# The MLP's output product in a two-layer encoder kernel: seven half-size products by Strassen's scheme in place of eight

## The chip, the cores and the metric

The kernel runs on one NeuronCore of a Trainium2 chip. The metric is device time in microseconds (us) of one execution; a run is one execution, and the median of three runs is shown. A profile is one further execution taken by the hardware profiler. Engines: PE is TensorE (matmuls), DVE is VectorE, ACT is ScalarE, POOL is GpSimd, SP is SyncE, which here only issues DMAs.

## The reference

Two post-norm layers over x (1024 tokens by 1024 features, float32). Each layer is a mixer (gated linear plus differential attention, or windowed attention), a cross-attention into a memory, and a gated MLP with a causal convolution of width 3 on its gate. The change is in the MLP, whose second matmul is the output product:

```python
def conv_ffn(x, w_in, conv_w, conv_b, w_out):
    g, u = jnp.split(x @ w_in, 2, axis=-1)
    g = causal_depthwise_conv(g, conv_w, conv_b)
    h = jax.nn.gelu(g.astype(f32)) * u.astype(f32)
    return h.astype(x.dtype) @ w_out
...
        h = conv_ffn(x, ffn_w_in[i], ffn_conv_w[i], ffn_conv_b[i], ffn_w_out[i])
        x = layer_norm(DEEPNORM_ALPHA * x + h, ln_g[i, 2], ln_b[i, 2])
```

Here h is 1024 x 2816 and w_out is 2816 x 1024, for each of two layers.

## The kernel before, in words

**Precision by splitting.** Every matmul operand is split into a high and a low part (`split`, lines 113 to 115: ACT casts the source to the high part at line 114, DVE subtracts it from the source at line 115), and each product of two tiles is three matmuls: high by high, high by low, low by high.

**The MLP's first half: the gate and up product.** The hidden width is 22 chunks of 128, numbered j (`FF = 22`). `ffn_gen` (from line 354) makes for each j the gate and the up rows by a Strassen scheme already: seven products named P1 to P7, each of 12 matmuls of 512 columns, so 84 matmuls for one j. `seq` fixes the order of the products; `prep` (operand sums on DVE at line 385, then a split) runs up to six products ahead of `prod` (matmuls, lines 419 to 421), held by eight operand tiles rb. `post` empties PSUM, applies the convolution (`tap`, line 431) and the gelu, and multiplies (line 466) into a hidden tile h of 128 x 1024. Two h buffers take turns; they, and other scratch, are parts ("slots") of `acc`, the tile that otherwise holds x. Line 468 stores each h to DRAM (`hid`). `load` (line 377) fetches two raw weight tiles for each j, two j ahead, into four tiles, as soon as the last split that reads the old ones is done.

**The second half: the output product.** `ffn` walks two groups g of 512 tokens. For each g it walks the 22 j: `out_prep` loads a row of w_out (512 KB) and half of hid[j] (256 KB), and splits both; then, for each of four token tiles, `mm` (lines 553 to 555) runs three matmuls for each of two halves of the columns: 24 matmuls of 512 columns for one (g, j). PSUM has eight banks; all eight hold sums through a group. `evac` adds the result to ALPHA * x, and a layer norm follows. The last `LAST = 5` j of the second group are taken tile by tile, so that the norms of the last four tiles lie beside matmuls.

**What sets the order.** The program is written in one sequence, but a scheduler places each engine's instructions by its own estimate of when they can run. So the order on an engine is not the order in the text: an instruction whose inputs are early stands early. Each engine, and SP's DMA queue, then works strictly in that order on the chip.

Of the kernel before, what the change touches and what calls it, by code (L numbers as in the profile page):

```python
# [8 lines left out]
F32 = mybir.dt.float32  # L9
F32R = mybir.dt.float32r  # L10
# [7 lines left out]
P = 128  # L18
# [47 lines left out]
class Net:  # L66
    def __init__(s, tc, ctx, I, wlist):
        s.tc, s.nc, s.I = tc, tc.nc, I
        nc = s.nc
        cp = ctx.enter_context(tc.tile_pool(name="const", bufs=1))  # L70
        s.ident = cp.tile([P, P], F32, name="ident")
        s.nhalf = cp.tile([P, 4], F32, name="nhalf")

        pad = cp.tile([P, 88], F32, name="pad")
        nc.gpsimd.memset(pad[:, 0:1], 0.0)
        s.xh = cp.tile([P, NK, T], F32R, name="xh")
        s.xl = cp.tile([P, NK, T], F32R, name="xl")
# [9 lines left out]
        nc.gpsimd.memset(s.tiny("pad2", 88, 1)[:, 0:1], 0.0)  # L87
# [268 lines left out]
    def ffn_gen(s, l):  # L356

        nc = s.nc
        FF = s.FF
        cw = s.sm.tile([P, FF, 4], F32, name="cw", tag="cw", bufs=1)  # L360
        nc.sync.dma_start(out=cw, in_=s.I["conv"][l])
        accf = s.acc.rearrange("p t d -> p (t d)")
# [74 lines left out]

        def post(j, b):
            x, q = X[j], j % 2
# [21 lines left out]
            else:  # L461
# [7 lines left out]
                del X[j], raw[j]  # L469

        load(0, 0)
        load(0, 1)
# [16 lines left out]
        for i, (j, b) in enumerate(seq):  # L489
# [2 lines left out]
                dd += [s.d2(), s.d2()]  # L492
            prod(j, b)
            post(j, b)
            ahead(min(i + 6, 8) if i < 4 else i + 6)
            if i in (1, 3):
                yield
            if j == FF - 1 and b == "P2":
                s.xs.close()
                s.open_x(s.GU)  # L500
                s.out_start(l)
            elif j == FF - 1 and b in ("P3", "P7", "P4"):
                s.out_prep(("P3", "P7", "P4").index(b))
        yield


    LAST = 5

    def out_start(s, l):
        s.bl, s.bn, s.bu = l, 0, {}  # L510
        s.bseq = [(g, j) for g in range(2) for j in range(s.FF)]

    def out_prep(s, upto):
        nc = s.nc
        while s.bn < len(s.bseq) and s.bn <= upto and s.R.n() >= 3:
            g, j = s.bseq[s.bn]
            s.bn += 1
            st = s.stg.tile([P, T], F32, name="st", tag="st")
            nc.sync.dma_start(out=st, in_=s.I["ffn_out%d" % s.bl][j * P:(j + 1) * P, :])
            c = s.fc()  # L520
            nc.sync.dma_start(out=c, in_=s.hid[j][:, 512 * g:512 * g + 512])
            w, lo, u = s.R.get(), s.R.get(), s.R.get()
            s.split(u[:, 0:512], u[:, 512:T], c)
            s.split(w, lo, st)
            s.bu[g, j] = (w, lo, u)

    def evac(s, t, ps, tot):

        if not isinstance(ps, list):
            return s.acc_add(t, ps, True, tot)  # L530
        tt = s.tiny("tt", 2)
        for hf in range(2):
            c = slice(hf * 512, hf * 512 + 512)
            s.nc.vector.scalar_tensor_tensor(out=s.acc[:, t, c], in0=s.acc[:, t, c], scalar=ALPHA, in1=ps[hf],
                                             op0=ALU.mult, op1=ALU.add, accum_out=tt[:, hf:hf + 1])
        s.nc.vector.tensor_tensor(out=tot, in0=tt[:, 0:1], in1=tt[:, 1:2], op=ALU.add)

    def ffn(s, l, out=None, keep=None):
        nc = s.nc
        FF, L = s.FF, s.LAST  # L540
        s.load_ln(l, 2)
        late = []

        def mm(t, ps, js):
            po = ps if isinstance(ps, list) else [ps[:, 0:512], ps[:, 512:1024]]
            sl = slice((t % 4) * P, (t % 4) * P + P)
            for hf, o in enumerate(po):
                c = slice(hf * 512, hf * 512 + 512)
                for j in js:
                    w, lo, u = s.bu[t // 4, j]  # L550
                    hh, hl = u[:, 0:512], u[:, 512:T]
                    z = dict(skip_group_check=True)
                    nc.tensor.matmul(o, hh[:, sl], w[:, c], start=j == 0, stop=False, **z)  # L553
                    nc.tensor.matmul(o, hh[:, sl], lo[:, c], start=False, stop=False, **z)  # L554
                    nc.tensor.matmul(o, hl[:, sl], w[:, c], start=False, stop=j == FF - 1, **z)  # L555
# [6 lines left out]
        for g in range(2):  # L562
            ps = [s.d2(), s.d2(), [s.s1(), s.s1()], [s.s1(), s.s1()]]
            for j in range(FF - (L if g else 0)):
                s.out_prep(g * FF + j)
                for i in range(4):
                    mm(4 * g + i, ps[i], [j])
                s.R.put(*s.bu.pop((g, j)))
                s.out_prep(g * FF + j + 4)
                if 2 <= g * FF + j < 10:  # L570
                    t = g * FF + j - 2
                    nc.sync.dma_start(out=s.acc[:, t, :], in_=s.xres[t * P:(t + 1) * P, :])
                if late and j >= 1:
                    t, tot = late.pop(0)
                    s.ln(t, tot)
                    done(t)
            if g == 0:
                for t in range(4):
                    tot = s.tot()
                    s.evac(t, ps[t], tot)  # L580
                    late.append((t, tot))
        s.out_prep(2 * FF)
        s.hold = False
        xq = list(range(6))
        for i in range(4):
            t = 4 + i
            mm(t, ps[i], range(FF - L, FF))
            if i == 3:
                for j in range(FF - L, FF):
                    s.R.put(*s.bu.pop((1, j)))  # L590
            s.w_emit()
            tot = s.tot()
            if out is not None:
                s.last_tile(t, ps[i], tot, out)
                continue
            s.evac(t, ps[i], tot)
            s.ln(t, tot)
            done(t)
            for _ in range(2 * i):
# [3 lines left out]
            s.xtq = xq + [6, 7]  # L603
        s.drop_ln()

    def last_tile(s, t, ps, tot, out):

        nc = s.nc
        s.evac(t, ps, tot)
        g = s.ln_gen(t, tot, 1 if t < NT - 1 else 2)  # L610
        mu = next(g)
        if s.lag:
# [1020 lines left out]
```

## Time and profile before

| | |
|---|---|
| median of three runs | 2806.81 us (2803.17 to 2809.97) |
| the profiled execution's own time | 2802.9 us |
| its span, first to last instruction | 2801.2 us |
| PE, DVE, ACT, POOL busy, share of the span | 98%, 65%, 43%, 4% |
| granted TensorE clock, mean | 0.993 |
| DMA, mean over the span | 100 GB/s |

A busy share is the share of the span in which the engine had an instruction running. Matmuls overlap one another (each is drawn as lasting 389 ns), so a busy PE says that PE never waited, and how fast it goes is read from the spacing of the matmuls. "Idle before, releaser" is the time an engine stood still before an instruction, and what let it go on.

### The profile page before, as it was taken

The page shows a single profiled execution, that of the slowest core. Times are in us where ns is not written, and L with a number is a line of the kernel's source. Part 1 is how long each engine was busy: PE and PEld are TensorE (multiplying, and loading weights), DVE is VectorE, ACT ScalarE, POOL GpSimd, SP SyncE. Part 2 cuts the span into 40 slices and gives each one's busy share as a digit, 9 for nine tenths or more (in the row PEclk, how much of TensorE's full clock was granted, in tenths as well). Part 3 has the DMA queues.
Part 4 walks back from the last instruction along what each step waited for, and adds up shares of the span by engine and source line. Part 5 has one row for each costly group of instructions (what it writes and reads, how often), then busy time and mean ns, then how long its engine had stood idle before and what let it go on. Part 6 is the DMA issues. An engine that isn't in the chain of part 4 may idle for free.

```text
span 2801.2 us, 38176 instructions
## 1 busy us (share of the span) xinstructions
PE 2740.6 (98%) x14616; PEld 2304.2 (82%) x14616; DVE 1819.5 (65%) x3359; ACT 1192.9 (43%) x2303; POOL 105.3 (4%) x115
## 2 busy tenths in 40 slices
PE   8999999999999999999999999999998999999998
PEld 7778887899987888888887777789996888888887
DVE  4547665755589777764446787575569777775354
ACT  4325554433245444433333566343336444443232
POOL 0000000100010000000000000000000000000010
PEclk9999999999999999999999999999999999999999
DMA  3113313422213222226453323332212222226452
GB/s 130 39 48 94 103 48 94 132 83 82 69 56 111 76 85 89 75 102 218 147 173 121 103 56 99 98 100 82 76 53 98 89 86 76 90 83 210 143 174 96
DMA packets 94473, 279.12 MB, mean 100 GB/s; under 512 B 15026, under 2 KB 15315, under 8 KB 94291
## 3 DMA queue, kind: packets, MB, share of 16 engines
q1 hardware_dynamic: 92928, 274.87, 30.6%
q8 instruction: 115, 1.88, 0.3%
q10 hardware_dynamic: 1362, 1.81, 0.2%
q14 instruction: 68, 0.55, 0.1%
HBM read 212.67 MB, written 40.89 MB: 91 GB/s over the span
## 4 chain that ended last, share of the span: by engine, by line
PE 74%; DVE 4%; ACT 1%; DMA 1%; issue 1%; POOL 0%; DVEq 0%; SPq 0%; ACTq 0%; POOLq 0%
PE d L419 6%; PE d L420 6%; PE d L421 6%; PE s L421 4%; PE s L420 4%; PE s L419 4%; PE s L553 3%; PE s L554 3%; PE s L555 3%; PE d L554 3%; PE d L553 3%; PE d L555 3%; PE s L261 2%; PE s L714 2%; PE s L716 2%; PE s L715 2%
## 5 line engine op out<-in xcount | busy, mean ns | idle before, releaser
L114 ACT CAST rb<-st 128x1024 fp32r<-128x1024 f32 (+2 forms) x179 | 159.2, 890 | 260.8 <-issue 84.4
L115 DVE TENSOR_TENSOR rb<-st,rb 128x1024 fp32r<-128x1024 f32 (+2 forms) x179 | 182.1, 1018 | 114.4 <-ACT rb L114 106.5
L419 PE MATMUL s<-xh,rb 128*128 128x512 f32 x528 | 205.7, 389 | 0.0
L421 PE MATMUL s<-xh,rb 128*128 128x512 f32 x528 | 205.4, 389 | 0.0
L420 PE MATMUL s<-xl,rb 128*128 128x512 f32 x528 | 205.4, 389 | 0.0
L148 PE MATMUL s<-xh,rb 128*128 128x512 f32 x416 | 166.1, 399 | 1.5 <-DVE xl L115 1.5
L149 PE MATMUL s<-xl,rb 128*128 128x512 f32 x416 | 162.9, 392 | 0.0
L150 PE MATMUL s<-xh,rb 128*128 128x512 f32 x416 | 162.8, 391 | 0.0
L164 POOL TENSOR_TENSOR lnrs<-lnrs,nhalf 128x1 f32<-128x1 f32 x48 | 70.9, 1482 | 2209.8 <-DVE lnrs L163 2209.8
L431 DVE SCALAR_TENSOR_TENSOR fc<-f,cw,fc 128x512 f32<-128x512 f32 x176 | 132.2, 751 | 31.4 <-ACT fc L429 28.7
L714 PE MATMUL s<-gu,xh 128*128 128x256 f32 x512 | 144.6, 282 | 0.0
L114 ACT CAST rb<-acc 128x512 fp32r<-128x512 f32 (+1 forms) x124 | 83.1, 671 | 144.2 <-PE d L420 128.0
L716 PE MATMUL s<-gu,xl 128*128 128x256 f32 x512 | 143.5, 280 | 0.0
L715 PE MATMUL s<-gu,xh 128*128 128x256 f32 x512 | 143.4, 280 | 0.0
L115 DVE TENSOR_TENSOR rb<-acc,rb 128x512 fp32r<-128x512 f32 (+1 forms) x124 | 92.4, 747 | 63.3 <-ACT rb L114 62.8
L261 PE MATMUL s<-xh,rb 128*128 128x512 f32 x448 | 128.7, 398 | 3.5 <-ACT xh L114 1.1
L419 PEld LDWEIGHTS s<-xh,rb 128*128 128x128 f32 x528 | 99.2, 188 | 20.6
L421 PEld LDWEIGHTS s<-xh,rb 128*128 128x128 f32 x528 | 99.1, 188 | 20.6
L420 PEld LDWEIGHTS s<-xl,rb 128*128 128x128 f32 x528 | 99.1, 188 | 20.6
L441 DVE TENSOR_TENSOR acc<-s,acc 128x512 f32<-128x512 f32 x120 | 82.3, 686 | 43.4 <-PE s L421 43.3
L114 ACT CAST rb<-tmp 128x512 fp32r<-128x512 f32 x88 | 54.7, 624 | 129.6 <-PE d L420 119.9
L115 DVE TENSOR_TENSOR rx<-st,rx 128x1024 fp32r<-128x1024 f32 x70 | 85.7, 1225 | 29.0 <-ACT rx L114 28.7
(406 smaller groups left out, 7837.7 us busy)
## 6 DMA issues: line engine op xcount, KB each, us to landing
st<-in_ffn_out_dram SPq DMA_DIRECT2D x88, 512.0 KB, 3.7
st<-in_ffn_in_dram SPq DMA_DIRECT2D x44, 512.0 KB, 3.5
hid<-acc SPq DMA_DIRECT2D x44, 512.0 KB, 2.6
fc<-hid SPq DMA_DIRECT2D x88, 256.0 KB, 2.7
st<-in_mem_kv_dram SPq DMA_DIRECT2D x32, 512.0 KB, 3.8
f<-in_ffn_in_dram SPq DMA_DIRECT2D x22, 512.0 KB, 3.5
acc<-in_ffn_in_dram SPq DMA_DIRECT2D x22, 512.0 KB, 3.5
st<-in_memT_dram SPq DMA_DIRECT2D x16, 512.0 KB, 3.6
```

The source lines that it names most:

```text
L114: s.nc.scalar.copy(out=hi, in_=src)
L115: s.nc.vector.tensor_tensor(out=lo, in0=src, in1=hi.bitcast(F32), op=ALU.subtract)
L261: nc.tensor.matmul(ps[hf], a[:, c], b[:, hf * 512:hf * 512 + 512], start=st, stop=sp)
L419: nc.tensor.matmul(o, h[:, k, :], bh[:, q, :], start=first and k == 0, stop=False, **z)
L420: nc.tensor.matmul(o, h[:, k, :], bl[:, q, :], start=False, stop=False, **z)
L421: nc.tensor.matmul(o, lo[:, k, :], bh[:, q, :], start=False, stop=k == 3, **z)
L553: nc.tensor.matmul(o, hh[:, sl], w[:, c], start=j == 0, stop=False, **z)
L554: nc.tensor.matmul(o, hh[:, sl], lo[:, c], start=False, stop=False, **z)
L555: nc.tensor.matmul(o, hl[:, sl], w[:, c], start=False, stop=j == FF - 1, **z)
L714: nc.tensor.matmul(o, s.xh[:, k, sl], gh, start=k == 0, stop=False)
L715: nc.tensor.matmul(o, s.xh[:, k, sl], gl, start=False, stop=False)
L716: nc.tensor.matmul(o, s.xl[:, k, sl], gh, start=False, stop=k == NK - 1)
```

## The change

The output product h @ w_out is cut in two in each of its three directions: tokens, hidden width (chunk m against chunk m + 11) and columns. Seven products of half-size blocks replace eight. With A for h and B for w_out, the products are P1 = A11 B11, P6 = S2 T2, P2 = A12 B21, P7 = S3 T3, P5 = S1 T1, P3 = S4 B22, P4 = A22 T4; the S are four sums of blocks of h, the T four sums of blocks of w_out.

Each product walks 11 chunks m, each chunk is 12 matmuls of 512 columns (four token tiles, three matmuls), and needs one block of A and one of B, loaded into one tile of 128 x 1024 and split once. The seven products use the eight PSUM banks in two sets of four (A and B in `ffn`), and `post` adds their parts into x.

The sums are made during the gate and up product, on GpSimd (`gsum`), eight for each m and so 88 for each layer, 128 x 512 each. Hidden chunks are now visited in pairs (m, m + 11), by the table `jo`. Four tiles `wr` receive blocks of w_out. Results go to DRAM (`sa`, `sb`) by SP, each store written two products behind its sum in the text.

```diff
-                nc.sync.dma_start(out=s.hid[j], in_=h)
...
+        wr = {(0, 0): slot(12), (0, 1): slot(13), (1, 0): s.p1x[0], (1, 1): s.p1x[1]}
+        WS = (3, 5, 7, 8, 9, 11, 13, 14, 15, 17, 19)
...
+        def gsum(dst, o, x, y, op=ALU.subtract):
+            nc.gpsimd.tensor_tensor(out=o, in0=x, in1=y, op=op)
+            stores.append((dst, o))
...
+        def side(j, b):
+            m = j // 2
+            if b == "P5":
+                if j:
+                    raw_store(j - 1)
+                if j and j % 2 == 0:
+                    h_sums(m - 1)
+                if j in WS:
+                    w_load(WS.index(j))
+            if b == "P4" and j in WS or b == "P1" and j - 1 in WS or b in ("P2", "P7") and j and j % 2 == 0:
+                s.sa_store(2)
+            if b == "P2" and j in WS:
+                w_sums(WS.index(j))
...
+        def h_sums(m):
+            d = s.sa[m]
+            a11, a21, a12, a22 = (x[:, c:c + 512] for x in hs for c in (0, 512))
+            s1 = s.fc()
+            gsum(d["S1"], s1, a21, a22, ALU.add)
+            gsum(d["S3"], a21, a11, a21)
+            gsum(d["S2"], a11, s1, a11)
+            gsum(d["S4"], a12, a12, a11)
...
+        def w_sums(m):
+            d = s.sb[m]
+            b11, b12, b21, b22 = wr.values()
+            gsum(d["T1"], b11, b12, b11)
+            gsum(d["T3"], b12, b22, b12)
+            gsum(d["T2"], b22, b22, b11)
+            gsum(d["T4"], b21, b21, b22)
...
-    LAST = 5
+    LAST = 7
+    OUTS = (("P1", "A11", (0, 0)), ("P6", "S2", "T2"), ("P2", "A12", (1, 0)), ("P7", "S3", "T3"), ("P5", "S1", "T1"),
+            ("P3", "S4", (1, 1)), ("P4", "A22", "T4"))
...
+            st = s.bst[s.bn % len(s.bst)]
+            nc.sync.dma_start(out=st[:, 0:512], in_=s.sa[m][a])
...
+            nc.sync.dma_start(out=st[:, 512:T], in_=w)
+            hi, lo = s.R.get(), s.R.get()
+            s.split(hi, lo, st)
...
+            for m in ms:
+                hi, lo = s.bu[p, m]
+                w, wl = hi[:, 512:T], lo[:, 512:T]
+                nc.tensor.matmul(ps[i], hi[:, c], w, start=first and m == 0, stop=False, **z)
+                nc.tensor.matmul(ps[i], hi[:, c], wl, start=False, stop=False, **z)
+                nc.tensor.matmul(ps[i], lo[:, c], w, start=False, stop=last and m == H - 1, **z)
...
+            if b == "P1":
+                for o in (right(i), left(t), right(t)):
+                    add(o, ps[i], ALPHA)
```

**SP's queue in the gate and up product.** This is SP's order in layer 0, early in the gate and up product, before and after; `in_ffn_in` loads are the raw weight tiles that PE's products need, `hid`, `saA`, `saS` and `sbT` are stores, `in_ffn_out` loads feed the T sums. Before:

```order
L468 DMA hid2_97<-acc_64 128x1024
L377 DMA st_7372<-in_ffn_in_dram 128x1024
L377 DMA st_7373<-in_ffn_in_dram 128x1024
L468 DMA hid3_98<-acc_64 128x1024
L377 DMA f0_4810<-in_ffn_in_dram 128x1024
```

After, one round of T sums (loads, then stores that wait for their sums), with the loads between:

```order
L520 DMA p1x1_7468<-in_ffn_out_dram 128x512
L385 DMA f0_4909<-in_ffn_in_dram 128x1024
L520 DMA p1x0_7467<-in_ffn_out_dram 128x512
L571 DMA sbT14_188<-acc_64 128x512
L571 DMA sbT34_190<-acc_64 128x512
L571 DMA sbT24_189<-p1x1_7468 128x512
L571 DMA sbT44_191<-p1x0_7467 128x512
L520 DMA acc_64<-in_ffn_out_dram 128x512 x2
L520 DMA p1x1_7468<-in_ffn_out_dram 128x512
L520 DMA p1x0_7467<-in_ffn_out_dram 128x512
L385 DMA acc_64<-in_ffn_in_dram 128x1024
```

The scheduler has moved the rounds of T sums far ahead of where the text has them: the stores of S4 for the first, second, third and fourth pair of chunks have 1, 15, 30 and 44 stores of T sums before them, so all of them stand ahead of the fourth of eleven pairs, and the raw loads stand behind stores that wait for sums.

**GpSimd's queue in the gate and up product.** There was nothing here before but one memset; now, in layer 0 between the first and the second pair's sums (fc is S1 of a pair, the rows that write p1x are T2 and T4):

```order
L483 TENSOR_TENSOR acc_64<-acc_64 128x512
L483 TENSOR_TENSOR acc_64<-p1x1_7468,acc_64 128x512
L483 TENSOR_TENSOR p1x1_7468<-p1x1_7468,acc_64 128x512
L483 TENSOR_TENSOR p1x0_7467<-p1x0_7467,p1x1_7468 128x512
L483 TENSOR_TENSOR fc_8742<-acc_64 128x512
L483 TENSOR_TENSOR acc_64<-acc_64 128x512
L483 TENSOR_TENSOR acc_64<-fc_8742,acc_64 128x512
```

Rounds of four T sums follow each other, with the four S sums of a pair between.

**DVE's queue where the last product begins.** In layer 0 the norms of the first token tiles (L182, L185 before; L185, L188 now) stand beside the last splits (L115; L118). Before, the last splits and the first of the last four tiles:

```order
L115 TENSOR_TENSOR rx7_10813<-st_12216,rx6_10812 128x1024
L115 TENSOR_TENSOR rb0_70<-st_12224,rb7_77 128x1024
L115 TENSOR_TENSOR rb5_75<-st_12262,rb4_74 128x1024
L205 SCALAR_TENSOR_TENSOR acc_64,tot_12270<-acc_64,d2_11634 128x1024
L115 TENSOR_TENSOR rb1_71<-st_12266,rb6_76 128x1024
```

After, with the norms of the first three tiles between the splits (tt8 rows: P3's last parts added from PSUM):

```order
L613 SCALAR_TENSOR_TENSOR acc_64,tt8_11224<-acc_64,d2_11980 128x512
L166 TENSOR_SCALAR lnrs_12360<-lnrs_12360 128x1
L185 SCALAR_TENSOR_TENSOR acc_64<-acc_64,lnmu_12359,f1_4910 128x1024
L118 TENSOR_TENSOR rx1_11140<-st_11146,rx0_11139 128x1024
L188 SCALAR_TENSOR_TENSOR acc_64<-acc_64,lnrs_12360,f2_4911 128x1024
L118 TENSOR_TENSOR rx3_11142<-rp0_11137,rx2_11141 128x1024
L166 TENSOR_SCALAR lnrs_12388<-lnrs_12388 128x1
L185 SCALAR_TENSOR_TENSOR acc_64<-acc_64,lnmu_12387,f1_4910 128x1024
L118 TENSOR_TENSOR rx5_11144<-rp1_11138,rx4_11143 128x1024
```

Seven splits of the last product now share DVE with four norms, where the norms of the first four tiles had a whole group of 22 steps before.

## Rows read from the trace of the kernel before

**Rows 1.** The page, part 1 (busy time) and part 2 (PE over 40 slices).
```profile
span 2801.2 us, 38176 instructions
PE 2740.6 (98%) x14616; PEld 2304.2 (82%) x14616; DVE 1819.5 (65%) x3359; ACT 1192.9 (43%) x2303; POOL 105.3 (4%) x115
```
**Rows 2.** Windows: gate and up product, then three of layer 0's output product.
```profile
1000.00:1020.00 20.00, 20.00 (x90) 16.54 (x89) 15.20 (x24) 8.66 (x15) 0.00 (x0) 1.00 0.24 79
...
1270.00:1300.00 30.00, 30.00 (x134) 24.85 (x133) 14.07 (x16) 9.63 (x12) 0.00 (x0) 1.00 0.90 312
1300.00:1340.00 40.00, 40.00 (x178) 33.13 (x177) 14.34 (x16) 12.57 (x16) 0.00 (x0) 1.00 0.42 142
...
1480.00:1510.00 30.00, 29.61 (x147) 23.70 (x146) 22.00 (x35) 13.63 (x21) 4.34 (x3) 1.00 0.30 106
```
**Rows 3.** Whom PE waited for, 860 to 1267 us (the whole answer).
```profile
PE d L419 <- ACT acc L448: 0.2, 1, 0.2
```
**Rows 4.** DVE by line, gate and up product, 860 to 1250 us.
```profile
L441 DVE TENSOR_TENSOR acc<-s,acc 128x512 f32<-128x512 f32 x57 | 39.1, 686 | 15.4 <-PE s L421 15.4
L115 DVE TENSOR_TENSOR rb<-acc,rb 128x512 fp32r<-128x512 f32 x55 | 37.7, 686 | 24.4 <-ACT rb L114 24.4
L466 DVE TENSOR_TENSOR acc<-fc,acc 128x512 f32<-128x512 f32 x42 | 28.8, 689 | 1.8
```
**Rows 5.** GpSimd's line 164: duration min/median/max; then the timeline around 1404 us.
```profile
L164 POOL TENSOR_TENSOR dms<-dms,nhalf x32: 537/542/1384, 238.0 to 510.8; 128x1 f32<-128x1 f32 x32
...
1403.62 1.27 DVE L182 SCALAR_TENSOR_TENSOR acc<-acc,lnmu,f 128x1024 f32<-128x1024 f32 x1
1403.85 3.19 POOL L164 TENSOR_TENSOR lnrs<-lnrs,nhalf 128x1 f32<-128x1 f32 x1 [2.20 <-DVE lnrs L163]
1404.82 0.68 DVE L115 TENSOR_TENSOR rx<-fc,rx 128x512 fp32r<-128x512 f32 x1
1405.42 1.21 DVE L115 TENSOR_TENSOR rx<-st,rx 128x1024 fp32r<-128x1024 f32 x1
1407.07 1.28 DVE L185 SCALAR_TENSOR_TENSOR acc<-acc,lnrs,f 128x1024 f32<-128x1024 f32 x1 [0.44 <-POOL lnrs L164]
```
**Rows 6.** GpSimd by line and form: its only wide instructions, memsets.
```profile
L1143 POOL MEMSET gaT<- 32x1024 f32 x1 | 0.9, 942 | 0.1
L1148 POOL MEMSET fc<- 128x128 f32 x1 | 0.2, 213 | 0.0
```
**Rows 7.** The page, part 6: issues, KB each (all of a group), us to landing.
```profile
st<-in_ffn_in_dram SPq DMA_DIRECT2D x44, 512.0 KB, 3.5
hid<-acc SPq DMA_DIRECT2D x44, 512.0 KB, 2.6
fc<-hid SPq DMA_DIRECT2D x88, 256.0 KB, 2.7
```
**Rows 8.** SP's timeline, 934 to 964 us; then DVE's around 1004 us.
```profile
943.24 0.33 SPq L377 DMA_DIRECT2D acc<-in_ffn_in_dram  x1
...
953.49 9.11 SPq L377 DMA_DIRECT2D st<-in_ffn_in_dram  x2
...
1004.69 0.69 DVE L385 TENSOR_TENSOR tmp<-st 128x512 f32<-128x512 f32 x1 [1.18 <-DMA st<-in_ffn_in_dram]
```
**Rows 9.** DVE and ACT by line, layer 0's output product, 1267 to 1520 us.
```profile
L115 DVE TENSOR_TENSOR rx<-st,rx 128x1024 fp32r<-128x1024 f32 x32 | 39.2, 1225 | 9.9 <-ACT rx L114 9.8
L185 DVE SCALAR_TENSOR_TENSOR acc<-acc,lnrs,f 128x1024 f32<-128x1024 f32 x8 | 10.1, 1277 | 0.9 <-POOL lnrs L164 0.9
L534 DVE SCALAR_TENSOR_TENSOR acc<-acc,s 128x512 f32<-128x512 f32 x8 | 5.2, 681 | 0.1
...
L114 ACT CAST rx<-st 128x1024 fp32r<-128x1024 f32 x30 | 31.4, 1046 | 3.8 <-DMA st<-in_ffn_out_dram 2.4 <-DVE rx L115 1.4
```
**Rows 10.** The end of the span: PE's last matmul, DVE's last instructions.
```profile
2792.05 0.39 PE L555 MATMUL s<-rb,rb 128*128 128x512 f32 x1
...
2796.34 1.41 DVE L185 SCALAR_TENSOR_TENSOR acc<-acc,lnrs,f 128x512 f32<-128x512 f32 x2
```

More of the change, by code (lines that the diff above doesn't have):

```diff
@@ L359, in ffn_gen @@
         FF = s.FF
+        H = FF // 2
+        jo = [m + H * i for m in range(H) for i in range(2)]
         cw = s.sm.tile([P, FF, 4], F32, name="cw", tag="cw", bufs=1)
@@ L513, in out_prep @@
     def out_prep(s, upto):
         nc = s.nc
-        while s.bn < len(s.bseq) and s.bn <= upto and s.R.n() >= 3:
-            g, j = s.bseq[s.bn]
+        while s.bn < len(s.bseq) and s.bn <= upto and s.R.n() >= 2:
+            p, m = s.bseq[s.bn]
             s.bn += 1
[L518 to L536, printed above, removed]
+            _, a, b = s.OUTS[p]
@@ L539, in ffn @@
         nc = s.nc
-        FF, L = s.FF, s.LAST
+        H, L = s.FF // 2, s.LAST
         s.load_ln(l, 2)
         late = []
[L544 to L555, printed above, removed]
+        tt = [s.tiny("tt8", 2, 8) for _ in range(NT)]
@@ new lines, in ffn, with add, mm @@
+        left, right = (lambda t, c=c: s.acc[:, t, c:c + 512] for c in (0, 512))
+        stt = nc.vector.scalar_tensor_tensor
+        def add(o, x, al=1.0, tot=None):
+            stt(out=o, in0=o, scalar=al, in1=x, op0=ALU.mult, op1=ALU.add, accum_out=tot)
+        def mm(ps, i, p, ms):
+            first, last = s.OUTS[p][0] in ("P1", "P5", "P6"), s.OUTS[p][0] in ("P2", "P3", "P4")
+            c = slice(i * P, i * P + P)
+            z = dict(skip_group_check=True)
+            for m in ms:
[4 more added lines that the diff above has]
+                nc.tensor.matmul(ps[i], lo[:, c], w, start=False, stop=last and m == H - 1, **z)
@@ L559, in done @@
             nc.sync.dma_start(out=dst[t * P:(t + 1) * P, :], in_=s.acc[:, t, :])
-        s.lag = None
[L562 to L565, printed above, removed]
-                for i in range(4):
[L567 to L575, printed above, removed]
-                    done(t)
[L577 to L581, printed above, removed]
@@ L582, in ffn, with total, post @@
-        s.out_prep(2 * FF)
+        def total(t):
+            tot = s.tot()
+            nc.vector.tensor_tensor(out=tot, in0=tt[t][:, 0:1], in1=tt[t][:, 1:2], op=ALU.add)
+            return tot
+        def post(b, ps, i):
+            t = 4 + i
+            if b == "P1":
+                for o in (right(i), left(t), right(t)):
+                    add(o, ps[i], ALPHA)
+            elif b == "P6":
+                add(right(i), ps[i])
+            elif b == "P2":
+                add(left(i), ps[i], ALPHA, tt[i][:, 0:1])
+            elif b == "P7":
+                add(right(t), ps[i])
+            elif b == "P5":
+                add(right(t), ps[i], 1.0, tt[t][:, 1:2])
+            elif b == "P3":
+                add(right(i), ps[i], 1.0, tt[i][:, 1:2])
+                late.append(i)
+            else:
+                add(left(t), ps[i], 1.0, tt[t][:, 0:1])
@@ new lines, in ffn @@
+        s.lag = None
+        A = None
+        B = [s.s1() for _ in range(4)]
+        for p, (b, _, _) in enumerate(s.OUTS):
+            if b in ("P1", "P5"):
+                A = [x[:, c:c + 512] for x in (s.d2(), s.d2()) for c in (0, 512)]
+            ps = B if b in ("P6", "P7", "P4") else A
+            for m in range(H - (L if b == "P4" else 0)):
+                s.out_prep(p * H + m)
+                for i in range(4):
+                    mm(ps, i, p, [m])
+                    if m == H - 1:
+                        post(b, ps, i)
+                s.R.put(*s.bu.pop((p, m)))
+                s.out_prep(p * H + m + 4)
+                if p == 0 and m in (2, 5):
+                    s.sa_store(2)
+                if p == 0 and m >= 2:
+                    for t in ((0,), (1,), (2,), (3,), (6,), (7,), (4,), (5,), ())[m - 2]:
+                        nc.sync.dma_start(out=s.acc[:, t, :], in_=s.xres[t * P:(t + 1) * P, :])
+                if late and m < H - 1:
+                    t = late.pop(0)
+                    s.ln(t, total(t))
+                    done(t)
@@ L583, in ffn @@
+        assert not late and not s.stores
+        s.out_prep(7 * H)
         s.hold = False
```

63 lines of the change are left out of this document (45 added, 18 removed).

## The prediction, made before the changed kernel had run

> **What bounds the kernel now.** I read the busy times first: PE is busy for 2740.6 of 2801.2 us, the next engine, DVE, for 65%, and GpSimd for 4% [rows 1]. Then the waits of PE: over a whole gate and up product it waited 0.2 us [rows 3]. Then the windows, for the pace: 178 matmuls of 512 columns lie in 40 us at a granted clock of 1.00, and as each is drawn 0.39 us long, the pace is (40 + 0.39) / 178 = 0.2269 us for each [rows 2]. So both MLP stages are bound by the number of matmuls, and a matmul taken away is worth 0.227 us, as long as what feeds PE keeps up.
>
> **Matmuls removed.** Before: 22 chunks x 8 tiles x 2 halves x 3 = 1056 for each layer. After: 7 products x 11 x 4 x 3 = 924. Over two layers 264 fewer, of the same shape: 264 x 0.2269 = **59.9 us saved**. This is all there is to gain; the rest of the working is about what is given back.
>
> **The output stage's feeding.** One chunk is now 12 x 0.2269 = 2.72 us of PE. It needs one cast of 1.05 us on ACT and one subtraction of 1.23 us on DVE [rows 9], two DMA issues of 0.33 us on SP [rows 8], and 2 x 256 KB of DMA. DMA moved 312 GB/s at a busy share of 0.90 [rows 2], so 347 GB/s full: 524 KB take 1.5 us. Every feeder has over a microsecond to spare, and loads stand four chunks (11 us) ahead of a landing of 2.7 us [rows 7]. The densest stretch is P1, which also takes in x: about 16 tiles' worth of 524 KB and 1.6 MB of late stores in 30 us are 333 GB/s, just under 347, so I cost it at nothing; if it doesn't fit, the four chunks of lead cover a lag of a few us. At P1's end DVE adds 12 parts from PSUM, 12 x 0.68 = 8.2 us [rows 9], against two or three chunks already split (5.4 to 8.2 us): nothing, up to 3 us a layer.
>
> **The norms in the last product.** Seven splits at 1.23 and three norms at 2 x 1.28 [rows 9] take DVE 16.3 us after P3 ends, while PE has four chunks, 10.9 us, and then tiles whose later chunks need the last splits; PE's new order takes two tiles' early chunks first, another 5 us. About 0.5 us a layer is left. At layer 0's end each of the last four tiles now gives 21 x 0.227 = 4.8 us of matmuls for a norm instead of 6.8, and DVE was already busy for 22.0 of 30 us there [rows 2]: I put down 1 us. Behind the last matmul the same chain of one addition and one norm follows as before (9 us to the end of the span) [rows 10]. Together **2 us given back**, bounds 0 and 8.
>
> **The sums on GpSimd.** 88 a layer, and the scheduler puts 43 of the T sums and 12 S sums between the first and the fourth pair of chunks: 55 in six chunks, nine for each. A chunk is 84 x 0.2269 = 19.1 us. No row shows such a sum. From below it costs what DVE takes for the same size, 0.69 us [rows 4]. From above: GpSimd's memsets grow by (942 - 213) / 896 = 0.81 ns an element [rows 6]; three streams of 512 make 1.25 us, plus the 0.54 of its smallest two-input instruction [rows 5], 1.8 us. I take 1.25 us.
>
> By the Trainium skill (GPSIMD Engine Reference, § 3.1) a two-input element costs about 2.6 cycles at 1.2 GHz, an estimate of 1.1 us; the sum would be the same.
>
> Two things can come of it. First, **DVE's time**. It is busy 15.2 of 20 us [rows 2], so 4.6 us of a chunk are free. Rows 5 show that the two engines get in each other's way: an instruction of 0.54 us on GpSimd lasted 3.19 us while three DVE instructions with two inputs in SBUF ran back to back, and ended 0.4 us behind them. DVE lost nothing there (1.27, 0.68, 1.21 us are its usual times), but that GpSimd instruction had one element to read. A sum reads 512, and while it reads, DVE may stand. DVE's loss for each sum lies between 0 and 1.8 us; with DVE busy 76% of the time a sum of 1.25 us displaces 0.95. Over six chunks: 55 x 0.95 = 52 us against 6 x 4.6 = 28 free and six products of lead before PE feels it, 6 x 2.72 = 16: 8 us for each layer.
>
> Second, **SP's queue**. It is in order, and raw loads stand behind stores that wait for sums, which DVE meets soon after: one load landed 1.2 us later than DVE wanted it even before [rows 8]. A round is four sums, then a store issued, and a load that lands in 2.7 us [rows 7]: 4s + 3.8 us for a sum of s. Two chunks hold 3.6 rounds and four S sums, 18.4 s + 13.7 us, against 38.1: even at s = 1.33. Stretched by DVE to 1.7, three pairs lose 21 us, less 16 of lead: 4 us a layer.
>
> Both eat the same lead, and a DVE that waits for a load leaves GpSimd free, so I take **10 us a layer**, between 8 and the sum of both.
>
> **Sum.** 2802.9 (the profiled execution) - 59.9 + 2 + 2 x 10 = 2765 us. The median of the runs shown lies 3.9 us above the profiled time; I leave the forecast at **2765**. Two runs of this kernel differ by about 0.2%, so less than that (5.6 us) counts as the same.
>
> **Rivals.**
> *Everything is hidden* (the lead and DVE's free time hold): 2802.9 - 59.9 + 3 = 2746. For it: DVE lost nothing in rows 5. Against it: nine sums a chunk against 4.6 free microseconds.
> *SP's queue is the bound*: sums stretch as the 3.19 us row did, to 2.1 us; then two chunks take 52.3 us of the queue, 14.2 too many, 43 over three pairs, 27 after the lead, 54 for two layers, less what a waiting DVE gives back, say half: 2803 - 60 + 2 + 40 = 2785. It decides from s = 1.33 + 16 / 55 = 1.6 us.
> *DVE becomes the bound, and the change is slower*: each sum takes the reading path for its whole length and DVE stands for 1.6 us. Then 55 x 1.6 = 88, less 28 and 16, is 44 a layer: 2803 - 60 + 2 + 88 = 2833. It turns slower than before from a loss of 1.33 us a sum, (44 + 29) / 55. For it: all of DVE's instructions in this stage but the additions from PSUM (line 441, first of rows 4) have two inputs in SBUF, the kind that held GpSimd up in rows 5. Against it: 1.6 is more than a sum is likely to last.
> The Trainium skill has this as a rule (SBUF — State Buffer, § Who interferes with whom): a DVE instruction with two SBUF inputs and a GpSimd one that reads SBUF exclude each other, and the second to issue waits for the whole of the first. The trace agrees for GpSimd as the second (3.19 us for 0.54); no row shows DVE as the second.
> That the matmuls are not fewer is no rival: PE's order holds 1848 of them where it held 2112.
>
> **Numbers.** Forecast (2752 to 2774) 0.42; everything hidden 0.19; SP's queue (2774 to 2801) 0.20; DVE the bound (above 2801) 0.15; the other 0.04 is a stall of the output stage (2774 to 2790). The range 2742 to 2803 leaves out most of the slower case and little below. Within 0.2% of before lies the edge between SP's queue and DVE as the bound, 0.03 of each: the same 0.06. Faster: 0.42 + 0.19 + 0.17 + 0.04 = 0.82. Slower: 0.12.
>
> **What would show it.** In the profile after: PE's spacing still 0.227 us in the output product, and 1848 matmuls there; the window from the first S sum to the fourth pair with a PE below full and waits for the splits behind it, while later chunks show 0; GpSimd's sums near 1.25 us alone and 1.5 to 2 beside DVE; DVE's two-input instructions stretched beyond 0.69, its PSUM ones not; raw loads issued later than 9 us apart. I am wrong if PE waits for the last product's splits for more than 2 us a layer, if P1 waits for DMA, or if sums last over 2 us.

## The result, and the profile after

The changed kernel took 2821.25 us (median; 2818.80 to 2823.52), the kernel before beside it 2806.26: a ratio of **1.0052, 95% interval 1.0038 to 1.0067**. By the bound of 0.2% it is **slower**, by 15 us, where 2765 (2742 to 2803) had been forecast. The profiled execution took 2823.5 us, with a span of 2821.8 against 2801.2 [rows 1].

First the output product itself. These are the first and the last of its matmuls on its first line, in layer 0 and in layer 1, before and then after (durations min/median/max in ns, then the first and last start):

```profile
L553 PE MATMUL d<-rx,rx x88: 389/389/396, 1267.5 to 1491.5; 128*128 128x512 f32 x88
L553 PE MATMUL s<-rb,rb x4: 389/397/400, 1498.2 to 1511.9; 128*128 128x512 f32 x4
...
L553 PE MATMUL d<-rx,rx x88: 389/389/393, 2552.6 to 2776.6; 128*128 128x512 f32 x88
L553 PE MATMUL s<-rb,rb x4: 389/389/389, 2781.4 to 2791.6; 128*128 128x512 f32 x4
```
```profile
L622 PE MATMUL d<-rx x108: 388/389/504, 1303.3 to 1487.3; 128*128 128x512 f32 x108
L622 PE MATMUL s<-rb x8: 389/394/486, 1503.2 to 1518.7; 128*128 128x512 f32 x8
...
L622 PE MATMUL d<-rx x108: 388/389/504, 2599.7 to 2783.3; 128*128 128x512 f32 x108
L622 PE MATMUL s<-rb x8: 389/389/397, 2799.2 to 2812.0; 128*128 128x512 f32 x8
```

It went from 1511.9 - 1267.5 = 244.4 to 1518.7 - 1303.3 = 215.4 us in layer 0, and from 239.0 to 212.3 in layer 1: **55.7 of the 59.9 us are there.** But it starts 35.8 us later in layer 0. From its end there to its start in layer 1 another 40.3 us were added (1081.0 against 1040.7). With 0.2 us more behind the last matmul that is the whole difference: 35.8 - 29.0 + 40.3 - 26.7 + 0.2 = 20.6 us of span. So the time was lost ahead of the output product, where PE had waited for next to nothing before [rows 3].

The windows tell in which part of the gate and up product. The columns are busy time and instructions of PE, PEld, DVE, ACT and POOL, the granted clock, the DMA share and GB/s. First the changed kernel's layer 0, from the start of the product on, and layer 1's product; then the kernel before:

```profile
860.00:900.00 40.00, 39.55 (x175) 32.30 (x173) 39.61 (x55) 20.90 (x34) 9.25 (x7) 1.00 0.35 119
900.00:1060.00 160.00, 135.16 (x549) 109.12 (x548) 132.11 (x152) 55.43 (x92) 78.94 (x53) 0.91 0.64 220
1060.00:1140.00 80.00, 80.00 (x355) 66.26 (x354) 67.57 (x93) 35.60 (x58) 12.21 (x8) 1.00 0.29 100
1140.00:1270.00 130.00, 130.00 (x576) 107.66 (x575) 109.91 (x149) 59.26 (x96) 22.54 (x15) 1.00 0.30 104
2140.00:2560.00 420.00, 392.53 (x1673) 320.55 (x1674) 358.52 (x467) 179.28 (x297) 120.46 (x80) 0.95 0.44 151
```
```profile
900.00:1060.00 160.00, 160.00 (x708) 132.48 (x707) 122.18 (x189) 72.78 (x118) 0.00 (x0) 1.00 0.25 82
2140.00:2560.00 420.00, 417.29 (x1841) 344.79 (x1840) 318.45 (x489) 193.26 (x313) 0.00 (x0) 1.00 0.28 92
```

All of layer 0's loss lies in the 160 us in which the T sums are crowded: 549 matmuls instead of 708, 159 x 0.2269 = 36 us. From 1060 us on, with four sums for each pair of chunks, PE is full again at a clock of 1.00. Of the 160 us PE is idle for 24.8. In the other 135.2 it does 549 x 0.2269 = 124.6 us of work, so 10.6 more go, mostly in matmuls at a lower clock (0.91 granted over the window).

Two things go wrong in that window at once. These are the waits (total, times, longest) of DVE and of PE in it, and of SP's queue from 885 us on:

```profile
DVE tmp L393 <- DMA st<-in_ffn_in_dram: 14.9, 3, 7.8
DVE acc L393 <- DMA acc<-in_ffn_in_dram: 10.6, 4, 3.9
```
```profile
PE s L427 <- DVE acc L449: 24.8, 6, 7.9
```
```profile
SPq L571 <- POOL acc L483: 61.7, 31, 5.3
SPq L571 <- POOL p1x L483: 18.9, 16, 1.4
```

**SP's queue.** Stores wait there for sums (line 571), and the raw loads stand behind them. DVE then waits 25.5 us for raw blocks (before: 3.3 us in the same window, none longer than 1.2), and PE waits 24.8 us for DVE's additions (line 449). The raw loads issued between 889 and 1039 us, of the kernel before and then of the changed one:

```profile
L377 SPq DMA_DIRECT2D st<-in_ffn_in_dram x8: 327/327/328, 915.4 to 1038.4; - x8
L377 SPq DMA_DIRECT2D f<-in_ffn_in_dram x4: 327/328/328, 896.6 to 1010.6; - x4
L377 SPq DMA_DIRECT2D acc<-in_ffn_in_dram x4: 327/328/328, 905.2 to 1019.4; - x4
```
```profile
L385 SPq DMA_DIRECT2D st<-in_ffn_in_dram x7: 328/377/432, 889.1 to 1038.5; - x7
L385 SPq DMA_DIRECT2D f<-in_ffn_in_dram x3: 328/328/333, 903.2 to 1000.1; - x3
L385 SPq DMA_DIRECT2D acc<-in_ffn_in_dram x3: 405/422/425, 914.1 to 1011.8; - x3
```

Thirteen loads have twelve steps: (1038.5 - 889.1) / 12 = **12.45 us a raw load**. A chunk of 19.06 us needs two, 9.53 each. The spacing by itself names no cause, since raw loads come late whenever PE is slow, for whatever reason; the waits above do.

**DVE held by the sums.** DVE by line and shape in 900 to 1060 us (busy, mean ns; then the idle time before):

```profile
L439 DVE SCALAR_TENSOR_TENSOR fc<-f,cw,fc 128x512 f32<-128x512 f32 x28 | 29.4, 1049 | 1.1 <-ACT fc L437 0.6
L118 DVE TENSOR_TENSOR rb<-acc,rb 128x512 fp32r<-128x512 f32 x18 | 17.0, 945 | 0.0
L474 DVE TENSOR_TENSOR acc<-fc,acc 128x512 f32<-128x512 f32 x14 | 14.7, 1046 | 1.1 <-DVE acc L449 0.8
L449 DVE TENSOR_TENSOR acc<-s,acc 128x512 f32<-128x512 f32 x21 | 14.3, 681 | 0.0
```

Those with both inputs in SBUF grew (686 and 689 ns to 945 and 1046 [rows 4]). The addition that reads PSUM stayed at 681. By the Trainium skill (SBUF — State Buffer, § Who interferes with whom) a DVE instruction with two SBUF inputs and a GpSimd instruction that reads SBUF exclude each other; this trace agrees, now with DVE as the one that waits.

How a late load gets through to PE is seen around 943 us. Timelines of SP, then DVE, then PE (start, duration in us; in brackets the idle time before and who ended it):

```profile
937.38 1.69 SPq L571 DMA_DIRECT2D sbT<-acc  x2
939.12 0.43 SPq L385 DMA_DIRECT2D st<-in_ffn_in_dram  x1
```
```profile
943.20 1.37 DVE L393 TENSOR_TENSOR tmp<-st 128x512 f32<-128x512 f32 x1 [7.80 <-DMA st<-in_ffn_in_dram]
944.50 1.74 DVE L118 TENSOR_TENSOR rb<-acc,rb 128x512 fp32r<-128x512 f32 x1
...
949.75 0.68 DVE L449 TENSOR_TENSOR acc<-s,acc 128x512 f32<-128x512 f32 x1
```
```profile
950.49 0.80 PE L427 MATMUL s<-xh,rb 128*128 128x512 f32 x1 [7.89 <-DVE acc L449]
951.08 0.63 PE L428 MATMUL s<-xl,rb 128*128 128x512 f32 x1
951.51 0.63 PE L429 MATMUL s<-xh,rb 128*128 128x512 f32 x1
```

The raw load goes out right behind two T stores. DVE stands 7.80 us at line 393, which prepares a block for a product well ahead. Behind it in DVE's order is the addition of line 449, which empties a PSUM bank, and PE waits 7.89 us for that. It is not short of split blocks: counted from DVE's splits and PE's products, three lay ready when it stopped, the one it used next since 927.62 us. It has no bank to write to. Then its matmuls stand 0.43 us apart (951.08 to 951.51) instead of 0.227.

### The profile page after: what moved, and what is told of

Same layout as the page of the kernel before. It is cut to its first block, busy times and chain, and to the rows that moved or that the text cites. A ratio compares the mean times of both kernels' runs of the same rounds, so it can differ in the third digit from the quotient of the medians.

```text
span 2821.8 us, 38833 instructions
## 1 busy us (share of the span) xinstructions
PE 2707.5 (96%) x14352; PEld 2266.2 (80%) x14352; DVE 1987.8 (70%) x3401; ACT 1213.4 (43%) x2281; POOL 373.8 (13%) x291
## 5 line engine op out<-in xcount | busy, mean ns | idle before, releaser
L118 DVE TENSOR_TENSOR rb<-st,rb 128x1024 fp32r<-128x1024 f32 (+2 forms) x177 | 183.7, 1039 | 109.3 <-ACT rb L117 103.3
L427 PE MATMUL s<-xh,rb 128*128 128x512 f32 x528 | 214.4, 406 | 46.8 <-DVE acc L449 46.8
L428 PE MATMUL s<-xl,rb 128*128 128x512 f32 x528 | 212.6, 403 | 0.0
L429 PE MATMUL s<-xh,rb 128*128 128x512 f32 x528 | 212.3, 402 | 0.0
L151 PE MATMUL s<-xh,rb 128*128 128x512 f32 x416 | 166.8, 401 | 3.0 <-DVE xl L118 3.0
L439 DVE SCALAR_TENSOR_TENSOR fc<-f,cw,fc 128x512 f32<-128x512 f32 x176 | 147.9, 841 | 22.8 <-ACT fc L437 20.1
L152 PE MATMUL s<-xl,rb 128*128 128x512 f32 x416 | 163.8, 394 | 0.0
L153 PE MATMUL s<-xh,rb 128*128 128x512 f32 x416 | 163.4, 393 | 0.0
L427 PEld LDWEIGHTS s<-xh,rb 128*128 128x128 f32 x528 | 103.7, 196 | 73.7 <-DVE acc L449 51.9
L266 PE MATMUL s<-xh,rb 128*128 128x512 f32 x448 | 128.2, 397 | 3.8 <-ACT xh L117 1.5
L483 POOL TENSOR_TENSOR acc<-acc 128x512 f32<-128x512 f32 x66 | 102.4, 1551 | 156.7 <-DMA acc<-in_ffn_out_dram 112.2
L429 PEld LDWEIGHTS s<-xh,rb 128*128 128x128 f32 x528 | 103.4, 196 | 22.4
L118 DVE TENSOR_TENSOR rb<-acc,rb 128x512 fp32r<-128x512 f32 (+1 forms) x124 | 108.6, 877 | 15.7 <-ACT rb L117 15.3
L266 PEld LDWEIGHTS s<-xh,rb 128*128 128x128 f32 x448 | 82.6, 189 | 25.4 <-issue 3.1
```

Of the source, the lines that this page charges most:

```text
L118: s.nc.vector.tensor_tensor(out=lo, in0=src, in1=hi.bitcast(F32), op=ALU.subtract)
L151: nc.tensor.matmul(ps, h[:, k, :], s.xh[:, k, t0:t1], start=k == 0, stop=False)
L152: nc.tensor.matmul(ps, h[:, k, :], s.xl[:, k, t0:t1], start=False, stop=False)
L153: nc.tensor.matmul(ps, l[:, k, :], s.xh[:, k, t0:t1], start=False, stop=k == NK - 1)
L266: nc.tensor.matmul(ps[hf], a[:, c], b[:, hf * 512:hf * 512 + 512], start=st, stop=sp)
L427: nc.tensor.matmul(o, h[:, k, :], bh[:, q, :], start=first and k == 0, stop=False, **z)
```

## The experiments

The theory after this reading was *crowding*: the scheduler had put eleven rounds of T sums into 160 us, and there SP's queue and DVE both had too little room. The rivals: every sum costs, wherever it stands; and, within the crowding, the queue alone or the held DVE alone.

**e1, the rounds spread out.** The loads of a round are ordered on SP behind the latest raw load written before them; nothing else in the text is changed.

```diff
-            nc.sync.dma_start(out=r, in_=s.I["ffn_in"][l, jo[j] + FF * up])
+            s.lastraw = nc.sync.dma_start(out=r, in_=s.I["ffn_in"][l, jo[j] + FF * up])
...
         def w_load(m):
-            for (i, k), b in wr.items():
-                nc.sync.dma_start(out=b, in_=s.I["ffn_out%d" % l][(m + H * i) * P:(m + H * i + 1) * P, 512 * k:512 * k + 512])
+            with s.tc.issue_after(s.lastraw.ins):
+                for (i, k), b in wr.items():
+                    nc.sync.dma_start(out=b, in_=s.I["ffn_out%d" % l][(m + H * i) * P:(m + H * i + 1) * P, 512 * k:512 * k + 512])
```

> Same work as the changed kernel; only the place of the T rounds differs: each round's four loads of w_out blocks are ordered behind the latest raw load that was written before them, so that one round of four T sums runs per two chunks j (38.1 us) instead of one per about 12 us between 890 and 1047 us of layer 0. In the changed kernel TensorE ran 554 matmuls between 900 and 1060 us where the kernel before ran 712, and 1673 against 1841 between 2140 and 2560 us: 326 matmuls of 0.2269 us, 74 us for both layers. Theory 'crowding' (the sums cost TensorE time only because eleven rounds run in 160 us): all of the 74 us but a few come back, 2748 to 2758 us, ratio 0.979 to 0.983; VectorE busy about 34 of each 38 us. Rival 'every sum costs' (each of the 88 sums of a layer takes about 0.4 us from TensorE wherever it stands): the time stays at 2805 to 2822 us.

2750.77 us, ratio **0.9814 (0.9798 to 0.9831)**: crowding was right, and this version beats both kernels. The two windows again:

```profile
900.00:1060.00 160.00, 160.00 (x707) 132.30 (x706) 148.50 (x187) 71.32 (x118) 54.93 (x36) 1.00 0.49 168
2140.00:2560.00 420.00, 418.84 (x1846) 345.91 (x1845) 375.26 (x461) 184.21 (x293) 137.22 (x88) 1.00 0.52 182
```

PE is full, DVE is busy for 93% of the first, and all 88 sums are still made. Output product: 215.8 us in layer 0, starting at 1267.4, as in the kernel before (1267.5).

**e4 and e3, short sums**, spread out as in e1 (e4) and crowded as in the change (e3). Both leave out all but one column of every sum but S1.

```diff
-            nc.gpsimd.tensor_tensor(out=o, in0=x, in1=y, op=op)
+            w = 512 if op == ALU.add else 1
+            nc.gpsimd.tensor_tensor(out=o[:, 0:w], in0=x[:, 0:w], in1=y[:, 0:w], op=op)
```

> Leaves work out as e3 does, with the rounds placed as in e1: the floor of the change, sums free and nothing crowded. Every theory expects 2741 to 2750 us (2801.2 less 264 matmuls of 0.2269 us and what lies around the span, and a few us for the norms that moved). e1 less this is what the 77 shortened sums of a layer cost when they are spread out: 'crowding' expects 0 to 8 us for both layers, 'every sum costs' 60 us.

> Leaves work out: the T sums and three of the four S sums work on one column of 512 instead of all; the loads, the stores, the instructions and the crowding of the rounds stay. Theory 'held': VectorE's stretch goes, so the time falls to 2745 to 2758 us. Theory 'queue': a round's chain of load, four sums, store loses its 6 us of sums and is some 6 to 7 us long, shorter than the 9.5 us between raw loads, so it falls to the same value; a time above 2780 us would speak against both, and for the transfers themselves (0.61 to 0.76 of the DMA engines busy in that window).

e4: 2747.08 us, ratio 0.9799 (0.9778 to 0.9820): the floor. e1 lies 3.7 us above it (their runs just overlap). e3: 2757.99 us, ratio 0.9841 (0.9822 to 0.9861): with short sums the crowding still costs 10.9 us. The window from 900 us, of e4, then of e3:

```profile
900.00:1060.00 160.00, 160.00 (x707) 132.50 (x706) 124.61 (x187) 72.94 (x119) 15.82 (x36) 1.00 0.49 167
```
```profile
900.00:1060.00 160.00, 157.17 (x691) 129.21 (x690) 118.02 (x183) 69.91 (x116) 22.66 (x56) 1.00 0.69 234
```

For the same 707 matmuls DVE is busy for 148.5 us in e1 and 124.6 in e4. One sum in eight is whole in both, so 31.5 of 36 differ: **0.76 us of DVE a sum**.

**e2 and e7, the queue relieved.** e2 issues the T rounds' loads and stores on GpSimd's queue; e7 issues the raw loads on ScalarE's.

```diff
-            stores.append((dst, o))
+            stores.append((dst, o, nc.gpsimd if dst.name.startswith("sbT") else nc.sync))
...
-                nc.sync.dma_start(out=b, in_=s.I["ffn_out%d" % l][(m + H * i) * P:(m + H * i + 1) * P, 512 * k:512 * k + 512])
+                nc.gpsimd.dma_start(out=b, in_=s.I["ffn_out%d" % l][(m + H * i) * P:(m + H * i + 1) * P, 512 * k:512 * k + 512])
...
-            dst, o = s.stores.pop(0)
-            s.nc.sync.dma_start(out=dst, in_=o)
+            dst, o, q = s.stores.pop(0)
+            q.dma_start(out=dst, in_=o)
```
```diff
-            nc.sync.dma_start(out=r, in_=s.I["ffn_in"][l, jo[j] + FF * up])
+            nc.scalar.dma_start(out=r, in_=s.I["ffn_in"][l, jo[j] + FF * up])
```

> The T rounds stay crowded, but their loads of w_out blocks and the T stores are issued on GpSimd's own DMA queue, so that the raw loads of the gate and up weights on SP's queue no longer stand behind them. Theory 'queue' (the raw loads come late, one per 12 us instead of one per 9.5, because SP's queue waits for the T rounds): VectorE's waits for raw blocks, 25.5 us between 900 and 1060 us of the changed kernel, go, and TensorE is fed again: 2750 to 2770 us. Rival 'held' (VectorE's operations are stretched beside the sums and VectorE is full in that window): its busy time per matmul stays as it is (129 us for 554 matmuls) and the time stays above 2795 us.

> Whole sums and crowded rounds; only the raw loads of the gate and up weights are issued on ScalarE's queue, so that no T store stands ahead of them. ScalarE then waits for each raw buffer, with its casts behind. Theory 'queue': raw loads come every 9.5 us, VectorE no longer waits for them, and what is left is VectorE's stretch: 129 us busy for 554 matmuls in the changed kernel is 0.233 us a matmul, 0.006 over the pace, 4 to 8 us a layer: 2755 to 2775 us. Theory 'held': the time stays above 2795 us. A confusion to look for: with nothing between them the T rounds may run ahead of the second pair's S sums, as in e2, and VectorE would then wait for those.

Both were slower than the change: 2865.71 us, ratio 1.0222 (1.0203 to 1.0241), and 2839.84, ratio 1.0137 (1.0120 to 1.0153). By the bounds set beforehand both fall to *held* (above 2795 us), but neither tells queue from held, since each only moved the wait into another engine's order. In e2 the T rounds ran ahead of S sums on GpSimd, and DVE waited for an S store to leave h (first row, 900 to 1060 us). In e7 ScalarE stood at raw loads with its casts behind (the others, 885 to 1060 us):

```profile
DVE acc L474 <- DMA saS<-acc: 14.8, 1, 14.8
```
```profile
DVE rb L118 <- ACT rb L117: 31.9, 9, 11.2
ACT f L460 <- DVE rb L118: 30.7, 4, 11.2
```

**e5, sums nearly as long but light.** This keeps the crowding and most of the length of a round, and takes away what holds DVE: every sum but S1 becomes five instructions of one column each, and the other columns are left out.

```diff
-            nc.gpsimd.tensor_tensor(out=o, in0=x, in1=y, op=op)
+            if op == ALU.add:
+                nc.gpsimd.tensor_tensor(out=o, in0=x, in1=y, op=op)
+            else:
+                for i in range(5):
+                    nc.gpsimd.tensor_tensor(out=o[:, i:i + 1], in0=x[:, i:i + 1], in1=y[:, i:i + 1], op=op)
```

> Leaves work out as e3 does, with the rounds crowded as in the changed kernel; but each shortened sum is five instructions of one column each, one after another, so that a round again takes about as long as with whole sums (0.27 us an instruction in e3, 1.4 us for five; a whole sum 1.3 to 1.6 us) while it reads only five columns of 512. Theory 'queue' (TensorE loses time because the raw loads stand on SP's queue behind stores that wait for a long round): raw loads again about 12 us apart between 890 and 1040 us, VectorE idle 20 us or more for them, and most of the 36 us a layer lost: 2800 to 2820 us. Theory 'held' (it is lost because the whole sums stretch VectorE's instructions): as e3, 2750 to 2765 us. In between, 2770 to 2795 us: each alone gives part, and only both together the whole.

2795.90 us, ratio 0.9979 (0.9969 to 0.9988): just above the middle band ("each alone gives part") and below the 2800 of *queue*. The window, DVE's waits in it, and two of its lines:

```profile
900.00:1060.00 160.00, 144.07 (x597) 116.95 (x597) 100.93 (x158) 60.69 (x100) 61.39 (x251) 0.94 0.66 223
```
```profile
DVE acc L393 <- DMA acc<-in_ffn_in_dram: 27.9, 4, 10.7
DVE tmp L393 <- DMA st<-in_ffn_in_dram: 23.3, 3, 10.0
```
```profile
L439 DVE SCALAR_TENSOR_TENSOR fc<-f,cw,fc 128x512 f32<-128x512 f32 x30 | 22.6, 753 | 3.7 <-ACT fc L437 3.2
L118 DVE TENSOR_TENSOR rb<-acc,rb 128x512 fp32r<-128x512 f32 x17 | 11.6, 684 | 0.0
```

DVE is at its usual durations, idle for 51 us waiting for raw blocks, and PE still loses 110 matmuls in the window. **Crowded long rounds in SP's queue are enough for most of the loss: 48.8 us over e4**, of the 74.2 by which the change lies above it. Of these, e3 has 10.9 from the crowding alone; 37.9 come with the rounds' length. The last 25 come with whole sums, but they are not simply DVE's share: five light instructions took 1.24 us on the mean (885 to 1060 us), a whole sum 1.50, so with 55 sums the change's rounds are also some 14 us longer in a layer. How the 25 divide is not shown.

**e6 and e8, one round for each chunk**, with whole sums (e6) and with e5's light ones (e8), raw loads ahead of the rounds as in e1.

```diff
-        WS = (3, 5, 7, 8, 9, 11, 13, 14, 15, 17, 19)
+        WS = tuple(range(2, 13))
```

> As e1, with one T round for each chunk j (19 us) in chunks 2 to 12 instead of one for two chunks: all whole sums, between e1 (38 us) and the changed kernel (about 12 us). Six sums then fall on a chunk; by e1 against e4 a sum takes 0.76 us of VectorE ((148.5 - 124.6) / 31.5 shortened sums in 160 us), so 4.6 us of the 4.6 free in a chunk: 'held' expects VectorE just full and 2752 to 2765 us; 'queue' expects two rounds and four S sums to fit into 38 us (12 x 1.56 + 2 x 3.8 = 26 us) and nothing lost against e1, 2748 to 2755 us. If the loss grows in proportion to the density of the rounds, it would be 2775 us or more.

> e6 with the light sums of e5 (it leaves the same work out): one T round for each chunk, the same places on SP's queue, the same loads and stores, sums as long but with five columns of 512. e6 lost 30 us against e1 while VectorE was busy 154.7 of 160 us and waited 1.3 us for raw loads. If that was VectorE being full from whole sums ('held'), nothing is left of it: 2745 to 2755 us. If it was the queue or the transfers at that density, 2770 us or more.

e6: 2780.41 us, ratio 0.9920 (0.9900 to 0.9939). e8: 2749.41 us, ratio 0.9810 (0.9793 to 0.9826). First e6, the window and DVE's wait for raw loads, then e8:

```profile
900.00:1060.00 160.00, 153.22 (x659) 125.52 (x658) 154.68 (x174) 65.38 (x110) 71.69 (x48) 0.98 0.58 197
```
```profile
DVE acc L393 <- DMA acc<-in_ffn_in_dram: 1.3, 4, 0.4
```
```profile
900.00:1060.00 160.00, 160.00 (x707) 132.48 (x707) 123.60 (x186) 73.07 (x119) 64.17 (x249) 1.00 0.66 222
```

In e6 the raw loads come in time and DVE is full (154.7 of 160 us, 3.9 of waits); in e8, with the same queue and the same transfers, nothing is lost. So **a DVE full of held instructions is enough too: 31.0 us at this density**. With 0.76 us a sum *held* had put e6 at 2765 at most; 2780 lies in the third band, a loss that grows with the density of the rounds. Scaled to e6's 659 matmuls, e8's DVE time is 123.6 x 659 / 707 = 115.2; the other 39.5 us over 44 sums (11 in 12 of 48 differ) are 0.90 each. Whether a sum costs more because DVE is fuller or because the sums stand denser, these runs don't tell.

**e9 and e10, four products of lead instead of six in the text**, in the changed kernel and in e1. The prediction had taken 16 us of lead off the loss in each layer.

```diff
-            ahead(min(i + 6, 8) if i < 4 else i + 6)
+            ahead(min(i + 6, 8) if i < 4 else i + 4)
```

> The changed kernel with its crowded rounds; the blocks of the gate and up product are prepared four products ahead of TensorE instead of six. Theory 'lead' (what VectorE falls behind comes off a store of split blocks first, as the prediction took it: six products, 16 us, in each layer): two products less are 5.4 us a layer, so about 11 us slower than the changed kernel, 2830 us or more. Rival 'in order' (VectorE's wait for a raw block holds up the additions queued right behind it, which TensorE needs now to get its PSUM banks back, however many blocks lie ready): no loss from it, 2812 to 2827 us.

> e1 with four products of lead instead of six. Control for e9, since VectorE there waits for next to nothing: 'in order' expects 2748 to 2755 us, as e1. If the lead is needed to carry TensorE over each burst of eight sums, it is slower by some microseconds: 2757 us or more.

2820.95 us, ratio 1.0067 (1.0049 to 1.0085), and 2750.48, ratio 0.9817 (0.9802 to 0.9833): nothing changed in either. By the letter that is *in order* (2812 to 2827 for e9). But e9 is no test of the lead, for the scheduler gave DVE nearly the same order again. Counted as above, 4 to 7 blocks were split at the start of every product between 900 and 1060 us in both kernels, 5.6 on the mean in the change and 5.7 in e9. DVE in e9 at the same late raw block:

```profile
943.87 1.33 DVE L393 TENSOR_TENSOR tmp<-st 128x512 f32<-128x512 f32 x1 [7.09 <-DMA st<-in_ffn_in_dram]
...
950.38 0.68 DVE L449 TENSOR_TENSOR acc<-s,acc 128x512 f32<-128x512 f32 x1
```

Between the two stand the same five instructions as in the change. e10's blocks, too, came hardly later than e1's (6.0 ahead against 6.3). What bears on the lead is the change's own trace: at each of PE's six waits in that window, 24.8 us in all, three to five split blocks lay ready when it stopped.

## Why the prediction was wrong

**Right.** The matmuls removed and their price. The output stage's feeding and the norms: 59.9 - 55.7 = 4.2 us given back, within the bounds of 0 and 8 for the norms (2 taken) and up to 3 a layer for the feeding (0 taken). PE waited 1.6 and 1.2 us of it, layer by layer, for additions from PSUM (line 613), and 0.2 us a layer for the last splits. The place of the loss: from the first S sum to the fourth pair, later chunks at full rate. The mechanisms: raw loads behind T stores, and DVE's two-input instructions stretched while its PSUM ones are not. (PE's waits were to be for splits, though, and were for additions.) The sum's length beside DVE (1.5 to 2 us forecast, 1551 ns the mean of its largest group). None of the three signs of being wrong came in the stages they watch: 0.2 us of waits for the last splits, no wait of P1 for DMA, no sum of the crowded window over 1.83 us. They watched none of what failed.

**Wrong by one term: the sums, 2 x 10 us taken.** They cost 35.8 us in layer 0, and in layer 1 what is left of 40.3 us after the 2.9 that e1 also shows there (1483.2 to 2526.8 us, 1043.6): 37.4. That is 73 against 20, and the top of the bounds was the sum of both halves, 12 a layer. Two steps of it failed:

- *"less 16 of lead"*, in both halves of the term. I let six split blocks absorb what DVE fell behind. But DVE works in order, and the instruction that waits, for a block needed later, stands ahead of the addition that PE needs now. Its 7.80 us came out as 7.89 at PE, with three split blocks (8.2 us of matmuls) lying ready. This step alone took 16 of the 24 us that I had for DVE and 16 of the 21 for the queue. (e9 was to test it and doesn't.)
- *SP's queue, "18.4 s + 13.7 us" for two chunks*. With the measured s = 1.49 (78.94 us for 53 sums in the window) this gives 41.1 us. Measured: four raw loads x 12.45 = 49.8. The 8.7 us between lie around the sums. GpSimd's waits, 885 to 1060 us:

```profile
POOL acc L483 <- DMA acc<-in_ffn_out_dram: 56.4, 10, 8.9
POOL acc L483 <- DMA p1x<-in_ffn_out_dram: 7.4, 5, 3.6
```

  Over the ten rounds that is some 6.2 us a round where I counted 3.8, and 3.6 rounds make 8.7 us of it. The landing was part of it, 3.6 us (the changed kernel's page) for 2.7. SP's queue also stood 15.4 us for DVE to free a raw buffer and 9.6 for h in these 175 us, waits that my sum left out: part of DVE's lateness comes back through the queue. (Twelve steps too long by 12.45 - 9.53 make 35.0 us: layer 0's loss again, seen at the raw loads.)

DVE's part was near in itself: 0.95 us a sum taken, 0.76 (e1) and 0.90 (e6) measured; the sum's length of 1.25 us is what it takes alone (1.26 to 1.30 between 936 and 943 us, while DVE waits). The Trainium skill's 2.6 cycles an element (GPSIMD Engine Reference, § 3.1) gave an estimate of 1.1 us, which is below every sum here. That I counted the two halves as sharing one loss fits what e5 and e6 show, that either one costs time without the other; how they share it in the change is not shown.

**The rivals.** *SP's queue the bound* (2785) named the cause that weighs most, and put half of its loss off as given back by a waiting DVE; e5, where the queue is alone, lies at 2796. Its sum is also wrong: half of 54 is 27 and not 40, which gives 2772, below its own band of 2774 to 2801. *DVE the bound* (2833) had the right side, but by 1.6 us a sum, which no run shows. *Everything is hidden* (2746) is what e1 comes to, 5 us above it, once the same sums stand elsewhere.

What stays open: the change with its crowding and whole sums but a queue in which raw loads never wait (e2 and e7 were meant as that and became something else), and a run in which DVE really splits fewer blocks ahead.

## What to carry to other kernels

Work put "beside" a stage by a scheduler stands where its inputs let it, not where the text spreads it: count what is due in the densest stretch, by queue and by engine, and if it doesn't fit there, pin it (here one ordering edge on the loads was worth 70 us). Blocks prepared ahead are a cushion only if the engine that falls behind has nothing else to deliver: in an engine that works in order, a wait for later work holds up what is needed now. Whether an edit to the text reached the chip has to be seen in the trace first, as e9's did not. And moving a blocked transfer to another in-order queue moves the block with it.

## What the runs showed of the hardware

- Sums that read 512 columns hold DVE; five instructions of one column each, 1.24 us together against 1.50, don't (e5: 753 and 684 ns for the lines that stood at 1049 and 945). A busy GpSimd alone doesn't hold DVE.
- One DVE instruction seems to have been held through several sums in a row. In e2 a tap of 0.75 us lasted 9.39, while six sums ran that left no gap (DVE, then the first and the last of the six):

```profile
952.04 9.39 DVE L439 SCALAR_TENSOR_TENSOR fc<-f,cw,fc 128x512 f32<-128x512 f32 x1
```
```profile
952.46 1.30 POOL L483 TENSOR_TENSOR fc<-acc 128x512 f32<-128x512 f32 x1
...
958.69 1.28 POOL L483 TENSOR_TENSOR p1x<-p1x,p1x 128x512 f32<-128x512 f32 x1
```

  It came free about 1.5 us after the last of them. In the change, where sums of a round depend on one another and have 0.1 us between them, the longest DVE instruction of these lines lasted 1.82 us. That the gaps are the reason is not shown.
- After PE's wait of 7.89 us eight matmuls ran at the 1.2 GHz level, 0.43 us apart, and those after the ninth at 2.4 GHz; the granted clock of 940 to 960 us was 0.83. Over the 160 us it was 0.91, which cost some 10 us on top of the 24.8 of waiting.
